# Rotary step of an interleaved diffusion trunk, split in two halves with its partner product behind the next chunk's projection

## The chip, the cores and the metric

The kernel runs on one core of one Trainium2 chip. The metric is the device time of one execution in microseconds (us). The kernel before has a median of 2652.2 us over 3 runs (2647.94 to 2653.35).

## What is computed

The reference is a trunk of four layers over 256 latent tokens and 256 context tokens of width 1024. Layers 0 and 3 mix tokens by differential attention, layer 1 by windowed grouped-query attention with sinks, layer 2 by a state-space scan; each mixer is followed by a gated feed-forward block. Only the rotary step of the attention layers is changed, and one multiplication in the differential softmax:

```
def apply_rope(t, cos, sin):
    t1, t2 = t[..., :half], t[..., half:]
    return jnp.concatenate([t1 * cs - t2 * sn, t2 * cs + t1 * sn], axis=-1)

q = apply_rope(qkv[..., :DA_WIDTH]..., cos, sin)      # latents only
k = apply_rope(qkv[..., DA_WIDTH:2 * DA_WIDTH]..., cos, sin)

p = jax.nn.softmax(s, axis=-1)
w = (p[:, :, 0] - lam * p[:, :, 1]).astype(v.dtype)
```

Context tokens get no rotation. In the last layer only latents are queried, but keys and values come from both streams.

## The kernel before

Activations lie feature-major: 8 chunks of 128 features by 512 tokens, the first 256 the context ("c"), the last 256 the latents ("l"). fp32 products are made of three matmuls on split operands: `uh`, `ul` are the rounded activation and its remainder, `wh`, `wl` the same of a weight. `load_w` fetches a 512 KB weight by DMA (SyncE's queue), rounds it on ScalarE (L261) and takes the remainder on GpSimd (L263).

An attention layer works in four groups of heads. A group has two key chunks and two query chunks (`qk_chunk`, a projection of 24 matmuls at L288 to L290 into a PSUM tile `mm` or `ar`), then the values (`v_tokens`, one token tile of 24 matmuls at L771 to L773 after the other), then the heads (`da_head`, `sw_head`). In layer 1 keys and values are made once, in group 0. In group 0 the two streams are projected apart (256 columns a matmul), later both at once (512 columns, except the queries of layer 3, which are latents only).

The latent half of a chunk is rotated by `rope`: ScalarE copies it to SBUF (`t`, L722), TensorE multiplies `t` by the matrix `rot` that swaps the partners (L724, into a PSUM tile `sm`), VectorE multiplies `t` by the cosine (L725) and the partner product by the sine (L726) and adds the two (L727, all in SBUF). `stack` then makes the operands of the score products: ScalarE writes the rounded halves (L701, L702), VectorE the remainder (L706 twice for keys, L712 for queries), and two DMAs move 64 partitions to the other half. The softmax of a head is L879 (maximum), L881 (exponential on ScalarE), L883, L884 (the second sum times minus lambda), L886, L887, and TensorE transposes the weights at L890. L471 to L475 are the normalisation of a head's output (`stat`), which ends in four transposes of `rs_y` at L475.

```
724         nc.tensor.matmul(rot[:, :HALF], self.cst["rot"], t, start=True, stop=True)
725         getattr(nc, self.ENG_ROPE).tensor_tensor(out=t, in0=t, in1=self.cst["cos"], op=AL.mult)
726         nc.vector.tensor_tensor(out=u, in0=rot[:, :HALF], in1=self.cst["sin"], op=AL.mult)
727         nc.vector.tensor_tensor(out=u, in0=u, in1=t, op=AL.add)
```

A scheduler orders each engine's instructions when the program is built. It mixes the next group's projections with the heads of the group at hand, so that a wait of one hides behind the other; once set, an engine's order is fixed. Tags of PSUM tiles have few buffers: `mm` 2 (and `ar` as a third in turn), `sm` 2 (in layer 3 `ad` as a third), `sc` 2. All 42 calls of `rope` (16 in layer 0, 10 in layer 1, 16 in layer 3) lie at 60 to 270, 760 to 900 and 2230 to 2380 us of the profiled execution.

Of the kernel before, what the change touches and what calls it, by code (L numbers as in the profile page):

```python
# [14 lines left out]
AL = mybir.AluOpType  # L15
AX = mybir.AxisListType

P = 128
D = 1024
KD = D // P  # L20
NT = 512
HALF = 256
# [12 lines left out]
def f32(ap):  # L35
    return ap.bitcast(F32)
# [139 lines left out]
class W:  # L176
    def __init__(self, h, l, kc, w):
        self.h, self.l, self.kc, self.w = h, l, kc, w


class Trunk:
# [28 lines left out]
    def __init__(self, ctx, tc, ins, outs, layers):  # L210
        self.tc, self.nc, self.ins, self.outs = tc, tc.nc, ins, outs
        self.layers = layers
        self.ctx = ctx
        pool = lambda n, **k: ctx.enter_context(tc.tile_pool(name=n, bufs=1, **k))
        self.main = pool("main")
        self.ps = pool("ps", space=bass.MemoryType.PSUM)
        self.dram = pool("dram", space=bass.MemoryType.DRAM)
        self.hs = None
        self.uid = 0
        self.poolw = set()  # L220
        self.wq, self.wloaded, self.wpos = [], {}, 0
        self.adaq = []
        self.adapend = []
        self.adaw = []
        self.extra, self.turn = None, {}
        self.arows = None

    def t(self, shape, tag, bufs=1, dt=F32, pool=None):
# [489 lines left out]
    def rope(self, src, scale):  # L718

        nc = self.nc  # L720
        t, u = next(self.vs), next(self.vs)
        nc.scalar.activation(t, src, AF.Copy, scale=scale)  # L722
        rot = self.psum("sm")
        nc.tensor.matmul(rot[:, :HALF], self.cst["rot"], t, start=True, stop=True)  # L724
        getattr(nc, self.ENG_ROPE).tensor_tensor(out=t, in0=t, in1=self.cst["cos"], op=AL.mult)  # L725
        nc.vector.tensor_tensor(out=u, in0=rot[:, :HALF], in1=self.cst["sin"], op=AL.mult)  # L726
        nc.vector.tensor_tensor(out=u, in0=u, in1=t, op=AL.add)  # L727
        return u

    def qk_chunk(self, wt, u, dst, kind, s):  # L730

        a, b = STREAMS[s]
        scale = 0.125 if kind == "q" else 1.0
        ps = self.psum("mm")
        self.lin(ps[:, : b - a], [(wt, range(KD))], 0, u[0], u[1], (a, b))
        if s != "l":
            self.stack(ps[:, :HALF], dst, kind, scale, slice(0, HALF))
        if s != "c":
            self.stack(self.rope(ps[:, b - a - HALF : b - a], scale), dst, kind, 1.0, slice(HALF, NT))

    def qk_tiles(self, tag, n, pool):

# [18 lines left out]
    def v_tokens(self, wv, u, dst, s):  # L761

        nc = self.nc
        a, b = STREAMS[s]
        mm = nc.tensor.matmul
        for tt in range(a // P, b // P):
            ps = self.psum("mm")
            tk = slice(tt * P, (tt + 1) * P)
            for k in range(KD):
                wt, kw = wv[k // 4], k % 4  # L770
                mm(ps[:, :HALF], u[0][k][:, tk], wt.h[:, kw, :], start=k == 0, stop=False)  # L771
                mm(ps[:, :HALF], u[1][k][:, tk], wt.h[:, kw, :], start=False, stop=False)  # L772
                mm(ps[:, :HALF], u[0][k][:, tk], wt.l[:, kw, :], start=False, stop=k == KD - 1)  # L773
            if dst[1] is None:
                nc.scalar.activation(dst[0][:, tt, :], ps[:, :HALF], AF.Copy)
            else:
                self.ctx_split(ps[:, :HALF], dst[0][:, tt, :], dst[1][:, tt, :])
# [83 lines left out]
    def da_head(self, hq, q, k, v, s, neg, pt4, pool):  # L861

        nc = self.nc
        a, b = STREAMS[s]
        nk = NT if s == "l" else HALF
        wth = self.t([P, 4, HALF], "wth", 1, F32R, pool=pool)
        wtl = self.t([P, 4, HALF], "wtl", 1, F32R, pool=pool)
        for qt in range(2):
            tk = slice(a + qt * P, a + (qt + 1) * P)
            mx = self.t([P, 2], "mx", 3)  # L870
            sm = self.t([P, 2], "sm", 3)
            pt = []
            pss = [self.psum("sc") for _ in range(2)]
            if self.PAIR:
                self.scores([ps[:, :nk] for ps in pss], q, k, range(2), tk, nk)
            for m, ps in enumerate(pss):
                if not self.PAIR:
                    self.scores([ps[:, :nk]], q, k, [m], tk, nk)
                nc.vector.tensor_reduce(out=mx[:, m : m + 1], in_=ps[:, :nk], axis=AX.X, op=AL.max, negate=True)  # L879
                p = next(pt4)  # L880
                nc.scalar.activation(p[:, :nk], ps[:, :nk], AF.Exp, bias=mx[:, m : m + 1], accum_out=sm[:, m : m + 1])  # L881
                pt.append(p)
            nc.vector.reciprocal(out=sm, in_=sm)  # L883
            nc.vector.tensor_tensor(out=sm[:, 1:2], in0=sm[:, 1:2], in1=neg, op=AL.mult)  # L884
            p0, p1 = pt[0][:, :nk], pt[1][:, :nk]
            nc.vector.tensor_scalar(out=p0, in0=p0, scalar1=sm[:, 0:1], scalar2=None, op0=AL.mult)  # L886
            nc.vector.scalar_tensor_tensor(out=p0, in0=p1, scalar=sm[:, 1:2], in1=p0, op0=AL.mult, op1=AL.add)  # L887
            tp = self.psum("sm")
            for kt in range(nk // P):
                nc.tensor.transpose(tp[:, kt * P : (kt + 1) * P], p0[:, kt * P : (kt + 1) * P], self.cst["ident"])  # L890
            src = tp[:, :nk].rearrange("p (k q) -> p k q", q=P)
            dh = wth[:, : nk // P, qt * P : (qt + 1) * P]
            dl = wtl[:, : nk // P, qt * P : (qt + 1) * P]
            nc.scalar.activation(dh, src, AF.Copy)
            nc.vector.tensor_tensor(out=dl, in0=src, in1=f32(dh), op=AL.subtract)
        ps = self.psum("sm")
        hc = slice(hq * P, (hq + 1) * P)
        n = nk // P
        for kt in range(n):
            self.mm3(  # L900
                ps[:, :HALF], v[0][:, kt, hc], v[1][:, kt, hc], wth[:, kt, :], wtl[:, kt, :],
                first=kt == 0, last=kt == n - 1,
            )
        return ps
# [104 lines left out]
    def sw_mixer(self, i, u, streams, pool, gate, after):  # L1009
        nc = self.nc  # L1010
# [10 lines left out]
        for g in range(4):  # L1021
            q = [self.qk_tiles("swq", self.SWQ, pool) for _ in range(2)]
            if g == 0:
                wk = [self.next_w(("swqk", i, c)) for c in range(2)]
                wq = [self.next_w(("swqk", i, 2 + c)) for c in range(2)]
                wv = [self.next_w(("swv", i, c)) for c in range(2)]
                for s in streams:
                    for c in range(2):
                        self.qk_chunk(wk[c], u, k[c], "k", s)
                    for c in range(2):  # L1030
                        self.qk_chunk(wq[c], u, q[c], "q", s)
                    self.v_tokens(wv, u, (v, None), s)
            else:
                for c in range(2):
                    self.qk_chunk(self.next_w(("swqk", i, 2 + 2 * g + c)), u, q[c], "q", "b")
            if g == 3:
                uo = self.u
                self.att_split(o, uo, range(6), streams)
            for s in streams:
                a, b = STREAMS[s]  # L1040
                n = 4 if s == "l" else 2
                for c in range(2):
                    wts = [
                        self.sw_head(4 * (2 * c + hr) + g, hr, q[c], k[c], s, sink, nsink, pt4, pool)
                        for hr in range(2)
                    ]
                    ps = self.psum("sm")

                    for kt in range(n):
                        for hr, wt in enumerate(wts):  # L1050
                            kv = 2 * c + hr
                            nc.tensor.matmul(
                                ps[64 * hr : 64 * hr + 64, :HALF], v[:, kt, 64 * kv : 64 * kv + 64], wt[:, kt, :],
                                start=kt == 0, stop=kt == n - 1, tile_position=(0, 64 * hr), skip_group_check=True,
                            )
                    nc.scalar.activation(o[2 * g + c][:, a:b], ps[:, :HALF], AF.Copy)
                if g == 3:
                    self.att_split(o, uo, (6, 7), s)
# [479 lines left out]
```

## Time and profile before

| what | value |
|---|---|
| median of 3 runs | 2652.2 us |
| profiled execution: its time, its span | 2648.17 us, 2646.2 us |
| TensorE matmul busy | 2495.8 us, 94% of the span |
| VectorE, ScalarE, GpSimd busy | 1538.5, 1212.5, 1113.6 us |
| mean granted TensorE clock | 0.983 |
| DMA | 353.29 MB, 134 GB/s on average |

TensorE is busy nearly throughout; the other engines have room on average. The span is the time from the first to the last instruction; some 2 us of the execution lie around it. A wait in the profile is idle time of an engine, put down to the instruction that ended it.

### The profile page before, as it was taken

What the parts mean: (1) busy time and instruction counts of PE and PEld (TensorE: products, weight loads), DVE (VectorE), ACT (ScalarE), POOL (GpSimd) and SP (SyncE); (2) the same over time, 40 slices, a digit from 0 to 9 for tenths busy, and PEclk for the clock granted to TensorE, in tenths of its full rate; (3) what the DMA queues carried; (4) which work ended last, traced back from release to release, by engine and by line L of the source; (5) the groups of instructions that cost most, each with busy time, mean ns of one, the idle gap of its engine ahead of it and who ended that gap; (6) DMA issues with size and microseconds to landing.
All of it is one profiled execution on the core that took longest, in us unless ns stands there. A gap on an engine that the chain in (4) does not pass through costs nothing. (4 is left out here: it accounts for less than half of the span.)

```text
span 2646.2 us, 37378 instructions
## 1 busy us (share of the span) xinstructions
PE 2495.8 (94%) x13570; PEld 2065.5 (78%) x13570; DVE 1538.5 (58%) x3797; ACT 1212.5 (46%) x2495; POOL 1113.6 (42%) x557
## 2 busy tenths in 40 slices
PE   7899999999989999999989899999999998997998
PEld 4777688888876688888877677678878887886997
DVE  3776658951467757961377777756673126766112
ACT  4555453222356753222356566645322225555443
POOL 3322035444241025444246556633544424433784
PEclk9999999999999999999999999999999998998999
DMA  8333427752141126752141121352684223333452
GB/s 319 126 102 129 144 90 250 259 179 96 64 150 45 53 72 235 254 172 96 52 139 57 64 76 56 101 179 77 201 310 159 97 76 128 97 93 121 162 186 76
DMA packets 108040, 353.29 MB, mean 134 GB/s; under 512 B 14032, under 2 KB 24656, under 8 KB 105808
## 3 DMA queue, kind: packets, MB, share of 16 engines
q1 hardware_dynamic: 107280, 349.57, 39.2%
q8 instruction: 107, 1.75, 0.3%
q10 hardware_dynamic: 576, 1.34, 0.1%
q14 instruction: 77, 0.63, 0.1%
HBM read 329.36 MB, written 11.53 MB: 129 GB/s over the span
## 5 line engine op out<-in xcount | busy, mean ns | idle before, releaser
L263 POOL TENSOR_TENSOR wl<-wr,wh 128x1024 fp32r<-128x1024 f32 x356 | 852.5, 2401 | 1339.2 <-ACT wh L261 1224.8
L261 ACT ACTIVATE wh<-wr 128x1024 fp32r<-128x1024 f32 x356 | 377.1, 1061 | 776.4 <-issue 278.6
L288 PE MATMUL mm<-uh,wh 128*128 128x512 f32 (+1 forms) x1184 | 423.7, 358 | 11.7 <-ACT uh L557 6.9
L289 PE MATMUL mm<-ul,wh 128*128 128x512 f32 (+1 forms) x1184 | 423.0, 357 | 0.6 <-DVE sublng L858 0.6
L290 PE MATMUL mm<-uh,wl 128*128 128x512 f32 (+1 forms) x1184 | 421.7, 356 | 0.0
L641 DVE TENSOR_TENSOR sc<-sc,sg 128x512 f32<-128x512 f32 (+1 forms) x100 | 57.6, 576 | 427.2 <-PE sc L290 420.3
L288 PE MATMUL sc<-uh,wh 128*128 128x512 f32 (+1 forms) x800 | 272.8, 341 | 0.7 <-DVE hid L644 0.7
L290 PE MATMUL sc<-uh,wl 128*128 128x512 f32 (+1 forms) x800 | 272.4, 341 | 0.0
L289 PE MATMUL sc<-ul,wh 128*128 128x512 f32 (+1 forms) x800 | 272.3, 340 | 0.0
L288 PEld LDWEIGHTS mm<-uh,wh 128*128 128x128 f32 x1184 | 228.2, 193 | 45.0 <-ACT uh L557 7.1
L289 PEld LDWEIGHTS mm<-ul,wh 128*128 128x128 f32 x1184 | 227.6, 192 | 30.4 <-issue 1.8
L290 PEld LDWEIGHTS mm<-uh,wl 128*128 128x128 f32 x1184 | 227.7, 192 | 29.9 <-issue 2.3
L298 PE MATMUL mm<-wh,hid 128*128 128x512 f32 x454 | 180.1, 397 | 0.9 <-DVE o L675 0.9
L300 PE MATMUL mm<-wl,hid 128*128 128x512 f32 x454 | 180.0, 397 | 0.0
L299 PE MATMUL mm<-wh,hid 128*128 128x512 f32 x454 | 179.7, 396 | 0.0
L288 PEld LDWEIGHTS sc<-uh,wh 128*128 128x128 f32 x800 | 152.1, 190 | 17.7 <-DVE hid L644 0.9
L290 PEld LDWEIGHTS sc<-uh,wl 128*128 128x128 f32 x800 | 151.9, 190 | 16.9
L289 PEld LDWEIGHTS sc<-ul,wh 128*128 128x128 f32 x800 | 151.8, 190 | 16.8
L387 DVE SCALAR_TENSOR_TENSOR sq<-wa,sm 128x512 f32<-128x512 f32 x224 | 145.4, 679 | 0.0
L263 POOL TENSOR_TENSOR wl<-wa,wh 128x1024 fp32r<-128x1024 f32 x49 | 117.7, 2403 | 59.7 <-ACT wh L261 57.0
L288 PE MATMUL ar<-uh,wh 128*128 128x256 f32 (+1 forms) x400 | 134.8, 337 | 1.9 <-ACT uh L557 1.9
L289 PE MATMUL ar<-ul,wh 128*128 128x256 f32 (+1 forms) x400 | 135.6, 339 | 0.0
(426 smaller groups left out, 5423.6 us busy)
## 6 DMA issues: line engine op xcount, KB each, us to landing
wr<-in_fin SPq DMA_DIRECT2D x154, 512.0 KB, 3.5
wa<-in_adat SPq DMA_DIRECT2D x144, 512.0 KB, 5.0
wr<-in_fout SPq DMA_DIRECT2D x77, 512.0 KB, 3.5
wr<-in_ssi SPq DMA_DIRECT2D x40, 512.0 KB, 3.5
wa<-in_adaw SPq DMA_DIRECT2D x36, 512.0 KB, 5.8
wr<-in_daqk SPq DMA_DIRECT2D x24, 512.0 KB, 3.9
wa<-in_fin SPq DMA_DIRECT2D x22, 512.0 KB, 3.5
wr<-in_sso SPq DMA_DIRECT2D x16, 512.0 KB, 3.5
```

The source lines that it names most:

```text
L261: nc.scalar.activation(h, raw, AF.Copy)
L263: eng.tensor_tensor(out=l, in0=raw, in1=f32(h), op=AL.subtract)
L288: mm(out, wh, ah[ka][:, a:b], start=j == 0, stop=False)
L289: mm(out, wh, al[ka][:, a:b], start=False, stop=False)
L290: mm(out, wl, ah[ka][:, a:b], start=False, stop=j == len(todo) - 1)
L298: mm(out, ah[ka][:, tk], wt.h[:, kw, :], start=j == 0, stop=False)
L299: mm(out, al[ka][:, tk], wt.h[:, kw, :], start=False, stop=False)
L300: mm(out, ah[ka][:, tk], wt.l[:, kw, :], start=False, stop=j == len(todo) - 1)
L387: nc.vector.scalar_tensor_tensor(out=self.t([P, D], "sq", 2)[:, :512], in0=w[:, x, :], scalar=1.0, in1=self.arows[r, x], op0=AL.mult, op1= ...
L641: nc.vector.tensor_tensor(out=pu[:, :w], in0=pu[:, :w], in1=sg[:, :w], op=AL.mult)
```

## The change

`rope` no longer returns a finished tile. It copies the latent half to SBUF as before, multiplies it by the cosine straight from the projection's PSUM tile (`w`, one instruction with the scale in it), and returns a function `rest`. That function holds the partner product, the product with the sine and the sum, both written in place to the PSUM tile; `stack` then reads the rotated chunk from PSUM. `qk_chunk` calls the previous chunk's `rest` and `stack` only after its own projection; the last query chunk's comes after the first token tile of the values, and in layer 1's later groups right behind the last query chunk. In the differential softmax the multiplication by minus lambda becomes a `tensor_scalar` with the factor as its scalar operand.

```diff
     def rope(self, src, scale):
 
         nc = self.nc
-        t, u = next(self.vs), next(self.vs)
+        t, w = next(self.vs), next(self.vs)
         nc.scalar.activation(t, src, AF.Copy, scale=scale)
-        rot = self.psum("sm")
-        nc.tensor.matmul(rot[:, :HALF], self.cst["rot"], t, start=True, stop=True)
-        getattr(nc, self.ENG_ROPE).tensor_tensor(out=t, in0=t, in1=self.cst["cos"], op=AL.mult)
-        nc.vector.tensor_tensor(out=u, in0=rot[:, :HALF], in1=self.cst["sin"], op=AL.mult)
-        nc.vector.tensor_tensor(out=u, in0=u, in1=t, op=AL.add)
-        return u
+        nc.vector.scalar_tensor_tensor(out=w, in0=src, scalar=scale, in1=self.cst["cos"], op0=AL.mult, op1=AL.mult)
+
+        def rest():
+            rot = self.psum("sm")[:, :HALF]
+            nc.tensor.matmul(rot, self.cst["rot"], t, start=True, stop=True)
+            nc.vector.tensor_tensor(out=rot, in0=rot, in1=self.cst["sin"], op=AL.mult)
+            nc.vector.tensor_tensor(out=rot, in0=rot, in1=w, op=AL.add)
+            return rot
+
+        return rest
...
-        if s != "c":
-            self.stack(self.rope(ps[:, b - a - HALF : b - a], scale), dst, kind, 1.0, slice(HALF, NT))
+        rest = self.rope(ps[:, b - a - HALF : b - a], scale) if s != "c" else None
+        self.turn_late()
+        if rest:
+            self.late = lambda: self.stack(rest(), dst, kind, 1.0, slice(HALF, NT))
+
+    def turn_late(self):
+        late, self.late = self.late, None
+        if late:
+            late()
...
             tk = slice(tt * P, (tt + 1) * P)
+            if tt == a // P + 1:
+                self.turn_late()
...
-            nc.vector.tensor_tensor(out=sm[:, 1:2], in0=sm[:, 1:2], in1=neg, op=AL.mult)
+            nc.vector.tensor_scalar(out=sm[:, 1:2], in0=sm[:, 1:2], scalar1=neg, scalar2=None, op0=AL.mult)
...
                     self.qk_chunk(self.next_w(("swqk", i, 2 + 2 * g + c)), u, q[c], "q", "b")
+                self.turn_late()
```

The built programs have as many instructions as before on SyncE, GpSimd, ScalarE, VectorE and TensorE, and differ in order only in and next to the three attention layers.

TensorE, layer 0, group 0, latents: the second query chunk is being projected into `mm`, and the partner product (L724, into `sm`) belongs to the first query chunk. Before:

```order
L290 MATMUL mm_144_730<-uh_13_84,wl_66_269 128x256
L288 MATMUL mm_144_730<-uh_13_84,wh_65_268 128x256
L289 MATMUL mm_144_730<-ul_14_85,wh_65_268 128x256
L724 MATMUL sm_143_720<-h_100_386,cst_att_93_370 128x256
L290 MATMUL mm_144_730<-uh_13_84,wl_66_269 128x256
L288 MATMUL mm_144_730<-uh_13_84,wh_65_268 128x256
```

In the change (the line numbers of the projection are one higher, the values' 15):

```order
L289 MATMUL mm_143_721<-uh_13_84,wh_65_268 128x256
L290 MATMUL mm_143_721<-ul_14_85,wh_65_268 128x256
L291 MATMUL mm_143_721<-uh_13_84,wl_66_269 128x256
L728 MATMUL sm_144_748<-h_100_386,cst_att_93_370 128x256
L786 MATMUL ar_145_757<-wh_68_274,uh_13_84 128x256
L787 MATMUL ar_145_757<-wh_68_274,ul_14_85 128x256
```

The partner product stood inside the next chunk's 24 projection matmuls, 11 behind their beginning; now it stands behind the last of them, in front of the first value tile.

VectorE, the same stretch, first and second key chunk. `h` is the SBUF scratch that `t`, `u` and `w` are cut from. Before:

```order
L726 TENSOR_TENSOR h_386<-sm_646,cst_att_370 128x256
L727 TENSOR_TENSOR h_386<-h_386 128x256
L706 TENSOR_TENSOR dk_389<-h_386,dk_387 64x256
L706 TENSOR_TENSOR dk_390<-h_386,dk_388 64x256
L725 TENSOR_TENSOR h_386<-h_386,cst_att_370 128x256
L726 TENSOR_TENSOR h_386<-sm_683,cst_att_370 128x256
L727 TENSOR_TENSOR h_386<-h_386 128x256
```

In the change:

```order
L724 SCALAR_TENSOR_TENSOR h_386<-ar_647,cst_att_370 128x256
L729 TENSOR_TENSOR sm_674<-sm_674,cst_att_370 128x256
L730 TENSOR_TENSOR sm_674<-sm_674,h_386 128x256
L707 TENSOR_TENSOR dk_389<-sm_674,dk_387 64x256
L707 TENSOR_TENSOR dk_390<-sm_674,dk_388 64x256
L1029 TENSOR_SCALAR nsink_6935<-sink_6934 128x16
L729 TENSOR_TENSOR sm_711<-sm_711,cst_att_370 128x256
L730 TENSOR_TENSOR sm_711<-sm_711,h_386 128x256
```

The cosine product of the second chunk (L724 of the change) has moved ahead of the first chunk's sine product; every instruction of the rotation now has one operand in PSUM.

ScalarE, the same stretch. Before:

```order
L722 ACTIVATE h_386<-mm_620 128x256
L261 ACTIVATE wh_1127<-wr_1126 128x1024
L701 ACTIVATE dk_387<-h_386 128x256
L702 ACTIVATE dk_388<-h_386 64x256
L722 ACTIVATE h_386<-ar_657 128x256
```

In the change:

```order
L723 ACTIVATE h_386<-mm_620 128x256
L262 ACTIVATE wh_1127<-wr_1126 128x1024
L723 ACTIVATE h_386<-ar_647 128x256
L262 ACTIVATE wh_1166<-wr_1165 128x1024
L702 ACTIVATE dk_387<-sm_674 128x256
L703 ACTIVATE dk_388<-sm_674 64x256
```

The second chunk's copy (L722, in the change L723) stood behind the first chunk's rounded halves; now it stands ahead of them.

## Rows read from the trace of the kernel before

**Rows 1.** The page's engines: busy us (share of the span) xinstructions.
```profile
PE 2495.8 (94%) x13570; PEld 2065.5 (78%) x13570; DVE 1538.5 (58%) x3797; ACT 1212.5 (46%) x2495; POOL 1113.6 (42%) x557
```
**Rows 2.** Layer 3's attention: length, busy us of PE, PEld, DVE, ACT, POOL, clock, DMA.
```profile
2220.00:2440.00 220.00, 186.75 (x1147) 161.81 (x1147) 146.42 (x319) 117.06 (x247) 83.35 (x44) 0.95 0.33 106
```
**Rows 3.** Waits of TensorE: line waited for, us in total, times, longest us.
```profile
PE sm L724 <- ACT h L722: 18.7, 15, 2.0
PE sm L475 <- DVE rs_y L442: 10.5, 7, 2.0
...
PE sm L890 <- DVE h L887: 5.8, 7, 1.4
...
PE ad L890 <- DVE h L887: 2.7, 1, 2.7
...
PE ad L724 <- ACT h L722: 2.0, 1, 2.0
```
**Rows 4.** Timeline, 73 to 79 us: start us, us, engine, line, out<-in [idle before <-releaser].
```profile
73.20 2.40 POOL L263 TENSOR_TENSOR wl<-wr,wh 128x1024 fp32r<-128x1024 f32 x1 [2.74 <-ACT wh L261]
...
73.62 2.26 DVE L727 TENSOR_TENSOR h<-h 128x256 f32<-128x256 f32 x1
...
75.92 0.42 ACT L701 ACTIVATE dk<-h 128x256 fp32r<-128x256 f32 x1 [2.79 <-DVE h L727]
...
77.76 0.37 ACT L722 ACTIVATE h<-mm 128x256 f32<-128x256 f32 x1
...
78.18 1.12 PE L724 MATMUL sm<-h,cst_att 128*128 128x256 f32 x2 [1.80 <-ACT h L722]
```
**Rows 5.** Instructions of L727, L726 and L712: duration ns min/median/max, first and last start, forms.
```profile
L727 DVE TENSOR_TENSOR h<-h x42: 417/425/2261, 68.6 to 2378.4; 128x256 f32<-128x256 f32 x42
...
L726 DVE TENSOR_TENSOR h<-sm,cst_att x38: 410/418/425, 68.1 to 2378.0; 128x256 f32<-128x256 f32 x38
...
L712 DVE TENSOR_TENSOR ql<-h,dq x16: 425/426/2414, 81.8 to 2379.3; 128x256 fp32r<-128x256 f32 x16
```
**Rows 6.** Busy time around three waits at L724 (columns as in rows 2; the clock fourth from the end).
```profile
74.00:78.30 4.30, 2.50 (x21) 2.29 (x21) 2.72 (x3) 2.16 (x4) 1.98 (x2) 1.00 0.65 215
78.40:81.70 3.30, 3.30 (x15) 3.12 (x15) 1.99 (x3) 0.31 (x1) 1.88 (x1) 0.50 0.36 82
...
774.70:778.00 3.30, 3.30 (x17) 3.24 (x16) 2.50 (x4) 1.10 (x3) 1.04 (x1) 0.50 0.37 105
...
2245.80:2249.10 3.30, 3.30 (x17) 3.30 (x17) 2.78 (x3) 0.66 (x2) 2.30 (x1) 0.50 0.11 29
```
**Rows 7.** Instructions of L884, L450 (a tensor_scalar of one column) and L1000, as rows 5.
```profile
L884 DVE TENSOR_TENSOR sm<-sm,neglam x48: 147/160/2218, 92.0 to 2407.9; 128x1 f32<-128x1 f32 x48
...
L450 DVE TENSOR_SCALAR rs_a<-rs_a x58: 204/214/217, 10.7 to 2639.5; 128x1 f32<-128x1 f32 x58
...
L1000 DVE TENSOR_SCALAR h<-h,sm x64: 342/476/2643, 790.9 to 918.0; 128x256 f32<-128x256 f32 x32, 128x512 f32<-128x512 f32 x32
```
**Rows 8.** Timeline of TensorE: two value matmuls of 256 columns, two projection matmuls of 512.
```profile
87.91 0.28 PE L772 MATMUL mm<-wh,ul 128*128 128x256 f32 x1
88.03 0.28 PE L773 MATMUL mm<-wl,uh 128*128 128x256 f32 x1
...
88.62 0.39 PE L288 MATMUL mm<-uh,wh 128*128 128x512 f32 x1
88.85 0.40 PE L289 MATMUL mm<-ul,wh 128*128 128x512 f32 x1
```
**Rows 9.** The stacked query's DMA (L715): time from issue to landing.
```profile
DMA to landing us min/median/max: 1.9/2.3/6.0
```
**Rows 10.** Timeline, layer 3: products of the second key and second query chunk, TensorE's wait.
```profile
2285.43 0.70 PE L724 MATMUL sm<-h,cst_att 128*128 128x256 f32 x2 [1.68 <-ACT h L722]
...
2289.05 0.70 PE L724 MATMUL sm<-h,cst_att 128*128 128x256 f32 x2 [0.35 <-ACT h L722]
```
**Rows 11.** What L724's engine waited for, us and times: L947 frees an `sm` tile.
```profile
  ACT o L947: 0.6, 3
```

More of the change, by code (lines that the diff above doesn't have):

```diff
@@ L225, in __init__ @@
         self.extra, self.turn = None, {}
+        self.late = None
         self.arows = None
```

## The prediction

> **What bounds the kernel now.** I read the engines' shares first: TensorE is busy for 94% of the span, VectorE for 58% [rows 1], so time is won where TensorE waits, and work taken off another engine counts only where TensorE waits for it. The stretches come next: in the attention of layer 3 TensorE is busy for 186.75 of 220 us [rows 2]; here, not in the feed-forward blocks, there is something to win. The list of waits says by what: TensorE waits at the rotary partner product L724 for ScalarE's copy L722, 15 times for 18.7 us and once for 2.0 us; these 20.7 us are the largest item that the change touches. Next to them stand the normalisation's transposes L475 (10.5 us) and the softmax's L890 (5.8 and 2.7 us) [rows 3].
>
> The timeline shows how such a wait comes about [rows 4]. GpSimd's weight remainder L263 starts at 73.20 and takes 2.40 us. VectorE's sum L727, with both inputs in SBUF, starts inside it at 73.62 and takes 2.26 us. ScalarE's L701 of the same chunk waits for that sum 2.79 us; behind it in ScalarE's order stands the next chunk's copy L722, which ends at 78.13, and TensorE, which came to L724 long before, has waited 1.80 us. The durations confirm the cause: L727 and L712, both with two SBUF inputs, have medians of 425 and 426 ns and maxima of 2261 and 2414, about the length of an L263; L726, with one input in PSUM, never exceeds 425 ns in 38 executions [rows 5]. So there are two faults here: VectorE is held up by GpSimd, and the product stands too early on TensorE for any delay to be absorbed.
>
> A longer wait also costs clock. After the 1.80 us wait the granted clock is 0.50 (1.2 of 2.4 GHz) from 78.4 to 81.7, where it was 1.00 before; the same level follows the two waits of 2.0 us, at 774.7 and 2245.8 [rows 6]. No other of these waits is followed so.
>
> **The change part by part.**
>
> *The product behind the next projection.* TensorE now meets it 24 matmuls later than the chunk's own end. A matmul starts 0.12 us after the last at 256 columns, 0.23 us at 512 [rows 8], so 2.9 or 5.5 us lie between; ScalarE's copy, 0.37 us long, has moved ahead of the previous chunk's L701 and no longer waits for the sum. The wait that needs most is the 2.0 us of rows 3, and before it the product already stood some matmuls into the next chunk. I take the whole 20.7 us as removed: **-20.7 us**. The bounds are 0 (all of it turns up elsewhere) and 20.7.
>
> *The clock.* Three stretches of 3.3 us at half clock did the work of 1.65 us each. Without a wait ahead of them I take them at full clock: 3 x 1.65 = **-5.0 us**; the bounds are 0 and 5.0, since the fall may come at another wait.
>
> *Sums and stacked parts from PSUM.* Each rotation keeps its count on VectorE: cosine, sine, sum, remainder. Now each has one PSUM input, like L726, so I expect 0.42 us each and no held-up ones. The profile has no sine product or sum written in place in PSUM; its price is bounded by L726's 410 and 425 ns [rows 5], and I take 418. What L727 and L712 lose to GpSimd goes from VectorE, but TensorE sees it only through the waits above: 0 beyond them.
>
> *Two readers on one bank.* The sine product, the sum, ScalarE's two halves and the remainder now follow each other on one `sm` tile: from the product to its release 0.7 + 0.42 + 0.42 + 0.4 + 0.4 + 0.42 (keys 0.84) = 2.8 to 3.2 us, where it was 0.7 + 0.42 + 0.42 = 1.5. With two buffers the second product after it wants the tile, two chunks later: 5.8 us of 256-column matmuls in group 0, about 5 us in layer 0's later groups, where the change puts 3 and then 20 projection matmuls of 512 columns between the first three products. So this is covered, with 2 us to spare. What a failing cover costs is the rival on the other side.
>
> *The last query chunk.* Its product now stands behind the first value tile, and its stacked part still has to land before the latents' scores: about 3 us to the DMA and 2.3 us to land [rows 9], 5.3 us. Three value tiles follow in the later groups (8.6 us), one in group 0 (2.9 us), where in layer 0 the context's scores come first; in layer 3 the first head needs only the first query chunk, whose product has two tiles behind it (5.8 us). Nothing for nearly all, up to 1 us once: 0.
>
> *Layer 3's later groups.* There the second key's product stood 11 matmuls into the second query chunk and still waited 1.68 us [rows 10]; it now stands at that chunk's beginning, 11 x 0.12 = 1.3 us earlier. It gains from projections that the new order starts earlier (seven of 512 columns, 1.6 us, before the first key's product instead of after it), so about 0.3 us may be left in each of three groups, here or at L475 behind it; the bounds are 0 and 1.7. **+1.0 us**.
>
> *Cover moved out of the heads.* In two of layer 0's groups six projections fewer stand before the last L475, 1.4 us each by 0.23 us a start. If TensorE waits there they are missed, if not they cost nothing: 0 to 2.8, and I take **+1.4 us**.
>
> *The multiplication by minus lambda.* L884 has a median of 160 ns and a maximum of 2218. A `tensor_scalar` on one column took 204 to 217 ns in 58 executions of L450, never held up. So it is 48 x 0.054 = 2.6 us more for VectorE, and the hold-ups go from this line. They do not go from the chain: directly behind stands L886, and L1000, the same operation on the same shapes, has been held up to 2643 ns [rows 7], so L886 inherits the wait. By L884's row alone the gain would reach the 2.7 us of TensorE's one long wait at L890 [rows 3]; by L1000's it is nothing. I take L1000's, and 0.05 us on each of 8 waits at L890: **+0.4 us**. The Trainium skill (SBUF — State Buffer, "Who interferes with whom") states that a VectorE instruction with two SBUF inputs contends with a GpSimd instruction that reads SBUF, and so does a `tensor_scalar` in its two-port mode: by it this edit moves the wait rather than ends it, the edits that read PSUM end it, and a sum from L884's row alone would be about 2.7 us lower. By that rule, the trace agrees: L727 at 2261 ns, L1000 at 2643, L726 at 425.
>
> The sum: -20.7 - 5.0 + 1.0 + 1.4 + 0.4 = -22.9 us. Against the profiled execution's 2648.2 us that is 2625.3. The median of the runs lies 4.0 us above this execution, which would give 2629.3; I forecast the middle, **2627 us**.
>
> **The rivals.**
>
> *Half comes back.* TensorE arrives earlier at the heads, but their softmax and normalisation chains on VectorE and ScalarE set the pace, and the time turns up at L475 and L890. For it: these lines already hold TensorE for 10.5 and 8.5 us [rows 3]. Against it: their inputs also come earlier, and VectorE is held up less. If 12 of the 25.7 us return, the gain is 11 and the time 2637 to 2641 us.
>
> *More than forecast.* VectorE's freed time also shortens L475 and L890, say by half of their 19 us: 2616 to 2620 us.
>
> *The rotary tile stays too long (slower).* The `sm` tile is shared with transposes, value products and normalisation. VectorE and ScalarE work in order; if the chain on the tile is stretched from 3 us beyond the 5 us between a product and the second one after it, TensorE waits at L728 or at a transpose. At 1.5 us for each of the 30 rotations outside group 0 that is 45 us against 25.7 gained: 19 slower, 2667 to 2671 us. Against it: L724 waited for an `sm` tile that L947 frees only 0.6 us in 3 times [rows 11]. It decides from a wait of 0.9 us per rotation (25.7 / 30).
>
> *No effect.* The products wait as before one chunk later, because ScalarE's copy is late for another reason (its order also carries the rounding of weights): 2648 to 2652 us.
>
> **How the numbers follow.** About 0.2%, 5.3 us, is what a measurement of this kernel can tell from no change. Forecast 0.55, half back 0.22, more 0.07, slower 0.08, no effect 0.08. Faster by over 0.2% are the first three, 0.84; within 0.2% 0.08; slower 0.08. The range takes in the forecast with its bounds (cover and layer 3 at their worst add 1.4 and 4.1 us, clock not won 5.0), the half-back case and most of the larger gain: 2614 to 2644. Outside lie the slower case, most of no effect, and the low end.
>
> **What would show it.** Right: waits of TensorE at the partner product of 2 us or less in all; none of the new sums above 0.5 us; no clock of 0.50 around the three places of rows 6; L886 with maxima above 2 us. Wrong: TensorE's waits at L475 and L890 (of the old numbering) grown by 10 us or more together; waits at the partner product put down to VectorE or to the release of `sm`; a span above 2640 us.

## The result and the profile after

The changed kernel takes 2624.4 us (median of 4 runs, 2623.08 to 2627.41) against 2652.8 us of the kernel before, run beside it: ratio 0.9892, 95% interval 0.988 to 0.9903. The profiled execution took 2624.96 us, with a span of 2623.1. The forecast was 2627 us, its range 2614 to 2644. The number came out; of the reasons a good part did not, as the runs below show.

The page's engines after, as [rows 1]:

```profile
PE 2489.5 (95%) x13570; PEld 2064.2 (79%) x13570; DVE 1511.0 (58%) x3797; ACT 1209.9 (46%) x2495; POOL 1114.4 (42%) x557
```

VectorE loses 27.5 us of busy time. The waits of TensorE after, as [rows 3] (the partner product is now L728, the normalisation's transposes L476, the transposes of the softmax weights L905):

```profile
PE ad L476 <- DVE rs_y L443: 7.2, 3, 2.4
...
PE sm L476 <- DVE rs_y L443: 5.6, 4, 1.9
PE ad L905 <- DVE h L902: 5.1, 4, 1.9
...
PE sm L728 <- ACT h L723: 4.5, 4, 1.4
...
PE sm L905 <- DVE h L902: 3.6, 6, 1.2
```

The product's 20.7 us are down to 4.5, but three waits of 2.4 us at L476, on tiles `ad`, are new: for these transposes `ad` stands in for `sm` in layer 3 alone. The sum L730, the remainder L713, the multiplication by minus lambda L899 and the scaling behind it L901, as [rows 5, 7] (the `sm` of L899 and L901 is the SBUF tile of the softmax sums, which shares its name with the PSUM tiles):

```profile
L730 DVE TENSOR_TENSOR sm<-sm,h x38: 416/432/433, 71.2 to 2359.9; 128x256 f32<-128x256 f32 x38
...
L713 DVE TENSOR_TENSOR ql<-sm,dq x12: 424/425/425, 78.8 to 2361.2; 128x256 fp32r<-128x256 f32 x12
...
L899 DVE TENSOR_SCALAR sm<-sm,neglam x48: 195/214/217, 86.7 to 2388.0; 128x1 f32<-128x1 f32 x48
...
L901 DVE TENSOR_SCALAR h<-h,sm x48: 343/478/2105, 86.8 to 2388.1; 128x512 f32<-128x512 f32 x32, 128x256 f32<-128x256 f32 x16
```

In this trace no operation that reads an operand from PSUM is held up, and L901 (L886 before, at most 484 ns there) has inherited what L899 lost; both as predicted. The clock, in stretches as [rows 2, 6] (busy time of PE, PEld, DVE, ACT, POOL; the clock is fourth from the end):

```profile
78.00:82.00 4.00, 4.00 (x34) 3.94 (x34) 2.05 (x5) 1.54 (x5) 2.11 (x1) 1.00 0.51 155
...
771.50:775.00 3.50, 3.50 (x21) 2.46 (x20) 1.95 (x7) 3.50 (x11) 0.00 (x0) 1.00 0.00 0
...
2253.40:2260.20 6.80, 5.56 (x24) 5.38 (x25) 3.50 (x9) 1.71 (x3) 0.64 (x1) 0.50 0.32 96
2200.00:2414.00 214.00, 186.41 (x1131) 162.95 (x1132) 137.63 (x298) 106.91 (x229) 81.60 (x44) 0.94 0.32 100
```

In layers 0 and 1 the two stretches at 0.50 of [rows 6] are gone. In layer 3 there is a longer one, and its attention is no shorter than before. The length of each attention is measured here from a transpose in the normalisation ahead of it (L541; L540 before; the same token tile in every kernel) to the first transpose of the one behind it. For layer 3, after:

```profile
2196.47 0.90 PE L541 MATMUL sm<-cst_base,sq 128*128 128x128 f32 x3 [5.67 <-ACT sq L537]
2413.53 0.90 PE L541 MATMUL ad<-cst_base,sq 128*128 128x128 f32 x4 [3.88 <-ACT sq L537]
```

That is 217.1 us. The same for every kernel of this study, from its profiled execution (us; "rest" is the span without the three; the time is the median of the runs):

| kernel | time | layer 0 | layer 1 | layer 3 | rest |
|---|---|---|---|---|---|
| before | 2652.8 | 291.4 | 200.7 | 210.5 | 1943.6 |
| after | 2624.4 | 273.5 | 190.2 | 217.1 | 1942.4 |
| e1 delay alone | 2642.2 | 289.7 | 193.9 | 208.3 | 1946.0 |
| e2 PSUM alone | 2625.3 | 282.6 | 194.6 | 202.5 | 1944.6 |
| e11 half of PSUM | 2629.6 | 284.6 | 193.7 | 204.1 | 1944.2 |
| e3 minus lambda undone | 2616.1 | 278.7 | 190.6 | 199.3 | 1945.7 |
| e4 no delay in layer 3 | 2619.5 | 273.8 | 190.4 | 206.4 | 1946.5 |
| e8 same order, other operation | 2629.9 | 274.4 | 190.4 | 217.7 | 1946.2 |
| e9 minus lambda alone | 2662.3 | 287.6 | 202.2 | 225.8 | 1948.9 |
| e5 inverse root in PSUM | 2612.1 | 272.7 | 191.3 | 201.5 | 1945.8 |
| e7 minus lambda in layer 0 only | 2610.6 | 272.5 | 190.7 | 199.1 | 1945.4 |
| e10 e5 and e7 | 2604.4 | 272.3 | 190.0 | 197.4 | 1942.5 |

The change gains 17.9 us in layer 0 and 10.5 in layer 1 and gives 6.6 back in layer 3. The rest differs by up to 6.5 us between kernels that are alike there; differences of a few us in the total are not explained by the stages.

How layer 3 gives time back stands in the timeline after, group 1 between its first and second key (all engines; start us, us):

```profile
2246.43 0.16 DVE L472 TENSOR_SCALAR rs_m<-sm 128x4 f32<-128x4 f32 x1
...
2246.76 2.40 POOL L264 TENSOR_TENSOR wl<-wa,wh 128x1024 fp32r<-128x1024 f32 x1 [7.63 <-ACT wh L262]
2246.88 2.31 DVE L435 TENSOR_SCALAR rs_y<-rs_m 128x4 int32<-128x4 int32 x1
...
2249.82 0.43 DVE L707 TENSOR_TENSOR dk<-mm,dk 64x256 fp32r<-64x256 f32 x1
...
2250.28 0.38 ACT L723 ACTIVATE h<-mm 128x256 f32<-128x256 f32 x1 [2.11 <-DVE dk L707]
...
2250.72 0.70 PE L728 MATMUL sm<-h,cst_att 128*128 128x256 f32 x2 [1.35 <-ACT h L723]
...
2251.69 2.35 POOL L264 TENSOR_TENSOR wl<-wr,wh 128x1024 fp32r<-128x1024 f32 x1 [2.53 <-ACT wh L262]
2251.85 2.21 DVE L442 TENSOR_TENSOR rs_a<-rs_a,rs_h 128x4 f32<-128x4 f32 x1
...
2254.43 0.15 DVE L443 SCALAR_TENSOR_TENSOR rs_y<-rs_a,rs_y 128x4 f32<-128x4 f32 x1
...
2254.64 1.11 PE L476 MATMUL ad<-cst_base,rs_y 128*128 128x128 f32 x4 [2.40 <-DVE rs_y L443]
```

L435 to L443 are the inverse root of the head normalisation (`rsqrt`), nine small VectorE operations. GpSimd's remainder L264 starts just before the first of them, and L435 takes 2.31 us in place of 0.17. Behind it in VectorE's order stands the remainder L707, for which ScalarE's copy L723 waits, and for that the partner product: 1.35 us. The next L264 holds up L442 for 2.21 us, and the transposes L476 wait 2.40. The same pair of waits comes in all three later groups, 11.3 us together. The stretch at half clock begins at 2253.4, inside the second wait of group 1.

### The profile page after: what moved, and what is told of

It reads as the page before. It is cut to its first block, busy times and chain, and to the rows that moved or that the text cites. A ratio compares the mean times of both kernels' runs of the same rounds, so it can differ in the third digit from the quotient of the medians.

```text
span 2623.1 us, 37393 instructions
## 1 busy us (share of the span) xinstructions
PE 2489.5 (95%) x13570; PEld 2064.2 (79%) x13570; DVE 1511.0 (58%) x3797; ACT 1209.9 (46%) x2495; POOL 1114.4 (42%) x557
## 5 line engine op out<-in xcount | busy, mean ns | idle before, releaser
L264 POOL TENSOR_TENSOR wl<-wr,wh 128x1024 fp32r<-128x1024 f32 x356 | 853.4, 2404 | 1297.2 <-ACT wh L262 1155.2
L289 PE MATMUL mm<-uh,wh 128*128 128x512 f32 (+1 forms) x1184 | 422.9, 357 | 11.3 <-ACT uh L558 6.9
L289 PE MATMUL sc<-uh,wh 128*128 128x512 f32 (+1 forms) x800 | 272.5, 341 | 0.8 <-DVE hid L645 0.6
L291 PE MATMUL sc<-uh,wl 128*128 128x512 f32 (+1 forms) x800 | 272.3, 340 | 0.0
L264 POOL TENSOR_TENSOR wl<-wa,wh 128x1024 fp32r<-128x1024 f32 x49 | 118.3, 2414 | 62.2 <-ACT wh L262 61.8
```

The costliest lines, as they stand in the source:

```text
L264: eng.tensor_tensor(out=l, in0=raw, in1=f32(h), op=AL.subtract)
L289: mm(out, wh, ah[ka][:, a:b], start=j == 0, stop=False)
L291: mm(out, wl, ah[ka][:, a:b], start=False, stop=j == len(todo) - 1)
```

## The experiments

A hold-up here is a VectorE operation that starts inside a GpSimd remainder and takes far longer than its median. Theory: hold-ups of VectorE by GpSimd are what costs, and the delay only makes room for them. Rivals: the product's place alone counts; the loss in layer 3 is the delay's; it is that of the multiplication by minus lambda, through its duration or through the order that the scheduler makes of it.

**e1, the delay alone.** The edits of `qk_chunk` and `v_tokens` stay; `rope` and L899 work as before:

```diff
+        def rest():
+            rot = self.psum("sm")
+            nc.tensor.matmul(rot[:, :HALF], self.cst["rot"], t, start=True, stop=True)
+            getattr(nc, self.ENG_ROPE).tensor_tensor(out=t, in0=t, in1=self.cst["cos"], op=AL.mult)
+            nc.vector.tensor_tensor(out=u, in0=rot[:, :HALF], in1=self.cst["sin"], op=AL.mult)
+            nc.vector.tensor_tensor(out=u, in0=u, in1=t, op=AL.add)
+            return u
```

> The delay alone: product and stack behind the next projection, but cosine, sine, sum and remainder from SBUF as before, and the multiplication by minus lambda as before. Theory 'placement' (the product stood too early on TensorE, the hold-ups of VectorE need not go): nearly the whole gain, 2624 to 2630 us, waits of TensorE at the product under 5 us although the sum still shows maxima of about 2.3 us. Theory 'lock' (only the end of the hold-ups by GpSimd counts): 2645 to 2653 us. If both parts are needed: 2632 to 2642 us, with waits at the product or at the scores left in between.

Measured: 2642.2 us, ratio 0.9965 (0.9952 to 0.9979), just past the upper end of "both needed". The sum and what waited for it (instructions of its line):

```profile
L730 DVE TENSOR_TENSOR h<-h x42: 410/426/2581, 71.6 to 2376.4; 128x256 f32<-128x256 f32 x42
...
  ACT dk L702: 33.8, 14
```

Delayed, the sum meets GpSimd more often: 17 of 42 are held up by over 0.5 us, before 7. TensorE's waits at the product fall to 8.4 us, but those at the scores grow (layer 3: 4.0 to 6.9 us; the 2.9 more are one wait for the DMA of a stacked query). Place alone does not do it.

**e2, the PSUM arithmetic alone.** L899 as before, and no delay:

```diff
-        self.turn_late()
         if rest:
-            self.late = lambda: self.stack(rest(), dst, kind, 1.0, slice(HALF, NT))
+            self.stack(rest(), dst, kind, 1.0, slice(HALF, NT))
```

> The PSUM arithmetic alone: cosine product from the projection's tile, sine product, sum and stacked parts in PSUM, but the product called at once as before; minus lambda as before. Theory 'placement': 2645 to 2653 us, TensorE still waits some 15 us at the product, now for the copy alone. Theory 'lock': 2624 to 2632 us, waits at the product under 5 us without any delay. Both needed: 2632 to 2645 us.

Measured: 2625.3 us, ratio 0.9903 (0.989 to 0.9917): as fast as the whole change. The product, still at its old place, waits 4.7 us:

```profile
PE sm L728 <- ACT h L723: 4.7, 14, 0.6
```

So 16 of the 20.7 us go without any delay. This is the "lock" theory's result.

**e11, half of it.** e2 with the sum written to SBUF, so that rounded parts and remainders come from there:

```diff
-            nc.vector.tensor_tensor(out=rot, in0=rot, in1=w, op=AL.add)
-            return rot
+            nc.vector.tensor_tensor(out=w, in0=rot, in1=w, op=AL.add)
+            return w
```

> The PSUM arithmetic alone without its second half: cosine product, sine product and sum read PSUM, but the sum is written to SBUF, and the rounded parts and the remainders are made from there, as before (no delay, minus lambda as before). In the kernel before, the held-up cosine products, sums and remainders lie at about 6, 13 and 18 us over their medians. If a hold-up counts for TensorE wherever it falls in the chain: about half of the 27 us, 2636 to 2642 us. If only the sum's hold-up reaches the next product: 2625 to 2630 us. If the remainder takes over the sum's hold-up (it is the next operation with two SBUF inputs): 2642 to 2652 us, with remainders held up more often than before.

Measured: 2629.6 us, ratio 0.9918 (0.9905 to 0.9932). The remainders are held up more than before: 16 of the 60 that read the sum, by 21.7 us over their median, where it was 9 and 17.3 us. One row for it:

```profile
L713 DVE TENSOR_TENSOR ql<-h,dq x16: 417/513/2411, 77.7 to 2360.3; 128x256 fp32r<-128x256 f32 x16
```

The cosine product and the sum carry some 22 of the 27 us; of the remainders' 21.7 us about 4 reach the time (e11 against e2). The time is that of the expectation's second case, though the third case's sign, more remainders held up, is there too.

**e3, minus lambda as before** (all else as in the change):

```diff
-            nc.vector.tensor_scalar(out=sm[:, 1:2], in0=sm[:, 1:2], scalar1=neg, scalar2=None, op0=AL.mult)
+            nc.vector.tensor_tensor(out=sm[:, 1:2], in0=sm[:, 1:2], in1=neg, op=AL.mult)
```

> The changed kernel with the multiplication by minus lambda as a tensor_tensor again. Prediction's step (the scaling behind it inherits the hold-up, so the edit moves a wait and saves none): within 2 us of the changed kernel, 2622 to 2626 us, with maxima of about 2.2 us back at this line and fewer held-up scalings. Rival (the edit ended hold-ups that TensorE waited for): 2 to 4 us slower, 2626 to 2629 us, and the transposes of the weights wait more.

Measured: 2616.1 us, ratio 0.9866 (0.9852 to 0.9879). Neither expectation: undoing the edit gains 8.2 us. Its hold-ups do behave as predicted:

```profile
L899 DVE TENSOR_TENSOR sm<-sm,neglam x48: 141/158/2201, 87.1 to 2375.5; 128x1 f32<-128x1 f32 x48
...
L901 DVE TENSOR_SCALAR h<-h,sm x48: 339/476/879, 88.7 to 2377.7; 128x512 f32<-128x512 f32 x32, 128x256 f32<-128x256 f32 x16
```

By the table the edit gains 5.2 us in layer 0 and costs 17.8 in layer 3. The order shows why it can: by the traces, the exchanged operation set aside, another instruction stands in 266 places of VectorE's order, 868 of TensorE's, 110 of ScalarE's and 4 of GpSimd's. Why the scheduler chose so is not shown. The timeline of e3 at the same place, group 1 of layer 3:

```profile
2250.52 0.17 DVE L435 TENSOR_SCALAR rs_y<-rs_m 128x4 int32<-128x4 int32 x1
...
2251.71 0.16 DVE L442 TENSOR_TENSOR rs_a<-rs_a,rs_h 128x4 f32<-128x4 f32 x1
...
2252.21 0.62 PE L476 MATMUL ad<-cst_base,rs_y 128*128 128x128 f32 x4
2252.55 2.39 POOL L264 TENSOR_TENSOR wl<-wa,wh 128x1024 fp32r<-128x1024 f32 x1 [6.50 <-ACT wh L262]
```

The inverse root runs in one go and is done before the next L264 begins. Neither product nor transposes wait.

**e4, no delay in layer 3's groups 1 to 3** (minus lambda as in the change):

```diff
             self.late = lambda: self.stack(rest(), dst, kind, 1.0, slice(HALF, NT))
+        if self.now:
+            self.turn_late()
...
+            self.now = g > 0 and not want_ctx
```

> The changed kernel, but in layer 3's groups 1 to 3 the product comes at once again. Theory 'the delay hurts there' (the second key's product stands at the start of the second query chunk with no cover and the normalisation's transposes right behind it, 3 x 1.4 and 3 x 2.4 us of waits that the kernel before did not have in this size): these waits fall to about the 6 us of before, and the time to about 2619 us. Rival 'GpSimd falls on the normalisation chain' (its instructions L435 and L442 are held up 2.3 and 2.2 us whatever the product does): the waits stay or move to other lines, and the time is 2622 to 2628 us.

Measured: 2619.5 us, ratio 0.9876 (0.9862 to 0.9889), exactly what "the delay hurts there" expected; the waits at L476 on `ad` are gone, the product waits 6.3 us in all. Yet e3, with the delay, has a shorter layer 3 (199.3 against 206.4), and e2, without delay and without the lambda edit, lies between (202.5). So the delay by itself does not hurt there; e4 changed the order too, and came upon a better one, in which L435 is still held up for 2.30 us in each of the three groups but L442 no longer. Its number fits a theory that falls.

**e8, the order of the change with another operation.** Whether order or operation costs:

```diff
-            nc.vector.tensor_scalar(out=sm[:, 1:2], in0=sm[:, 1:2], scalar1=neg, scalar2=None, op0=AL.mult)
+            nc.vector.scalar_tensor_tensor(out=sm[:, 1:2], in0=sm[:, 1:2], scalar=neg, in1=self.cst['ones'][:, 0:1], op0=AL.mult, op1=AL.mult)
```

> The changed kernel with the multiplication by minus lambda as a scalar_tensor_tensor whose second tensor is a column of ones in SBUF: the order of every engine stays word for word that of the changed kernel but for this operation's name, while the operation has two SBUF inputs again. Theory 'order' (the edit costs because the scheduler puts the normalisation's chain where GpSimd's remainders hold it up): about 2624 us, with three waits of 2.4 us at the normalisation's transposes in layer 3. Theory 'instruction' (a tensor_scalar with a scalar operand is the slow thing, by its length or by whom it passes the hold-up to): about 2616 us, without these waits.

Measured: 2629.9 us, ratio 0.991 (0.9898 to 0.9923). In the traces no engine's order differs from the change's but for this operation. It has two SBUF inputs again and is held up itself, L901 takes 804 ns at most, and the three waits stay:

```profile
L899 DVE SCALAR_TENSOR_TENSOR sm<-sm,neglam,cst_base x48: 199/219/1957, 87.1 to 2393.4; 128x1 f32<-128x1 f32 x48
```

```profile
PE ad L476 <- DVE rs_y L443: 7.2, 3, 2.4
```

Layer 3 takes 217.7 us, as in the change: the order costs there, not the operation. (Its 5 us over the change lie for the most part in the "rest" and are not explained.)

**e9, minus lambda alone on the kernel before** (the change's edit of that line, nothing else).

> The kernel before with nothing but the multiplication by minus lambda as a tensor_scalar. If the edit has a price of its own wherever it stands: 2658 to 2662 us (8 us more, as in the changed kernel). If its price is that of one order of the changed kernel, which the rotary step's place made: 2648 to 2655 us, or either way by a few us, with another pattern of waits at the normalisation's transposes.

Measured: 2662.3 us, ratio 1.0032 (1.0019 to 1.0044). Again layer 0 gains (3.8 us) and layer 3 loses (15.3), by three waits, longer still:

```profile
PE ad L475 <- DVE rs_y L442: 13.3, 3, 4.4
```

In each of these groups the inverse root again runs into two remainders: L434, its first operation here, takes 2.35 us, and L440 2.29. So the bad order came with this edit in both kernels, with the rotary step's change and without it.

**e5, the inverse root from PSUM** (minus lambda and delay as in the change). Mean, half mean and products lie in free columns of the sums' tile, and the squares are taken in two steps, so that no operation reads two SBUF tiles:

```diff
+            tt(out=a, in0=m, in1=y, op=AL.mult)
+            tt(out=a, in0=a, in1=y, op=AL.mult)
+            stt(out=b, in0=a, scalar=-10.0 / 3, in1=y, op0=AL.add, op1=AL.mult)
+            tt(out=a, in0=a, in1=b, op=AL.mult)
+            stt(out=y, in0=y, scalar=5.0, in1=a, op0=AL.mult, op1=AL.add)
+            tt(out=a, in0=mh, in1=y, op=AL.mult)
+            tt(out=a, in0=a, in1=y, op=AL.mult)
+            stt(out=y, in0=a, scalar=1.5 * 0.375, in1=y, op0=AL.add, op1=AL.mult)
...
+        if div == 128:
+            m, *sp = (ps[:, 8 * x : 8 * x + 2 * n] for x in range(1, 4))
```

> The changed kernel (minus lambda as a tensor_scalar in both layers) with the head normalisation's inverse root rewritten so that none of its operations reads two SBUF tiles: its mean, half mean and products lie in free columns of the PSUM tile of the sums, one operation more. Theory 'GpSimd on the normalisation chain': no operation of the chain exceeds 0.3 us, the waits of layer 3's groups 1 to 3 at the second key's product (1.4 us) and at the transposes (2.4 us) are gone, and the time is 2606 to 2614 us. Rival 'place' (the second key's product and the transposes stand too early on TensorE whatever VectorE is held up by): waits of over 1 us stay at both lines and the time is 2619 to 2625 us.

Measured: 2612.1 us, ratio 0.9842 (0.9826 to 0.9857). Layer 3 takes 201.5 us, 15.6 less. The first operation, with its input in PSUM in the heads and in SBUF in layer 2's four:

```profile
L435 DVE TENSOR_SCALAR rs_y<-sm x12: 143/157/161, 101.6 to 2380.1; 128x4 int32<-128x4 int32 x12
L435 DVE TENSOR_SCALAR rs_y<-rs_m x4: 162/1256/2346, 1458.3 to 1717.6; 128x4 int32<-128x4 int32 x4
```

The chain still meets the remainders, as the timeline of layer 3's group 1 shows (L446 is its last operation, L490 the transposes):

```profile
2248.18 2.40 POOL L264 TENSOR_TENSOR wl<-wa,wh 128x1024 fp32r<-128x1024 f32 x1 [7.64 <-ACT wh L262]
...
2248.30 0.15 DVE L435 TENSOR_SCALAR rs_y<-sm 128x4 int32<-128x4 int32 x1
...
2252.86 0.15 DVE L446 SCALAR_TENSOR_TENSOR rs_y<-sm,rs_y 128x4 f32<-128x4 f32 x1
...
2253.16 0.62 PE L490 MATMUL ad<-cst_base,rs_y 128*128 128x128 f32 x4
```

L435 starts 0.12 us into L264, as in the change, and takes 0.15 us. In the three groups 21 of the chain's operations start inside a remainder, none takes over 171 ns, and no wait is left at the product or at L490. So it is not a luckier order that helps here. Both that and e7 (below) remove the loss in layer 3, one by taking the chain out of GpSimd's reach, the other by its place: the mechanism is shown from two sides.

**e7, minus lambda as a tensor_scalar in layer 0 only** (in layer 3 as before):

```diff
+            if self.ts_lam:
+                nc.vector.tensor_scalar(out=sm[:, 1:2], in0=sm[:, 1:2], scalar1=neg, scalar2=None, op0=AL.mult)
+            else:
+                nc.vector.tensor_tensor(out=sm[:, 1:2], in0=sm[:, 1:2], in1=neg, op=AL.mult)
```

> The changed kernel with the multiplication by minus lambda as a tensor_scalar in layer 0 and as a tensor_tensor in layer 3. By the stages of the runs so far the edit gains 5.2 us in layer 0 (273.5 us of attention against 278.7) and costs 17.7 in layer 3 (217.0 against 199.3). If the two are independent: 2616.1 - 5.2 = about 2611 us, which is faster than every kernel so far. If layer 0's difference is not the edit's, but chance of the order: about 2616 us.

Measured: 2610.6 us, ratio 0.9841 (0.9827 to 0.9854), as expected.

**e10, e7 with e5's inverse root.**

> The changed kernel with minus lambda as a tensor_scalar in layer 0 only and with the inverse root of the head normalisation reading PSUM. If the two win the same hold-ups (the three places of layer 3 that each of them freed): no faster than the better one alone, 2609 to 2612 us. If the rewritten root wins something of its own in layer 0 and at the last group: 2603 to 2607 us.

Measured: 2604.4 us, ratio 0.9828 (0.9814 to 0.9841), the fastest of all: 47 us under the kernel before, run beside it. In layer 0 the last wait at the normalisation's transposes (here L490; 1.9 us in e7) goes too; what is left lies in layer 2, whose root still reads SBUF:

```profile
PE sm L490 <- DVE rs_y L454: 3.6, 3, 1.6
```

Its stages are 0.2 to 1.7 us shorter than e7's, the rest 2.9, and the runs overlap (2604.16 to 2610.18 against 2609.86 to 2613.06), so how much over e7 is its own stays open.

## Why the prediction was right, and where it was not

For the balance, each attention's length is split into TensorE's gaps of over 0.06 us, the time lost at half clock (half of the time at 0.50 outside these gaps) and what remains; sums over layers 0, 1 and 3:

| kernel | length | gaps | lost clock | remainder |
|---|---|---|---|---|
| before | 702.6 | 61.3 | 16.3 | 625.0 |
| e2 | 679.7 | 42.1 | 11.7 | 625.9 |
| e3 | 668.6 | 37.5 | 10.9 | 620.2 |
| after | 680.8 | 45.5 | 16.7 | 618.6 |

- *The product behind the next projection, -20.7.* Right for the rotary step without the lambda edit: e3 waits 0.2 us there, once. But the cause was given mostly to the place; by e2 the PSUM arithmetic removes 16 us of it, and by e1 the delay alone 12. The change as a whole keeps 4.5 us, more than twice the 2 us set as a sign.
- *The clock, -5.0.* Right in e3 (10.9 against 16.3, 5.4 less), wrong in the change: 16.7, no less than before, since layer 3's new waits bring stretches of their own.
- *PSUM arithmetic, 0 beyond these waits.* The price of the operations was right (432 ns against 418). "0 beyond" was too small: of the 22.9 us that e2 gains in the three attentions, 16 are the product's waits, 4.6 the clock, and 3 lie in other gaps (the remainder takes back 0.9). Both parts of the rotary edit (e3) gain 34.0 us there where 25.7 were expected: 3.1 of the 8.3 more are other gaps, 4.8 are the remainder of the table, which is not explained.
- *Two readers on one bank, 0.* Right: no kernel's product waits more than 0.3 us for an `sm` tile to be released, and the rival built on it is out.
- *Layer 3's later groups, +1.0.* The place was right, the cause and size wrong. The product waits 1.4 us there, not 0.3, and the transposes 2.4 us, but with the same delay e3 has neither.
- *Cover moved out of the heads, +1.4.* Not seen: layer 0's waits at the last transposes fell from 6.9 us to 4.9 in e3 and 1.9 in the change.
- *Minus lambda, +0.4.* **This step failed**: the edit costs 8.2 us. That the hold-up passes to the next operation was right (L901 at 2105 ns). The Trainium skill (SBUF — State Buffer, "Who interferes with whom") states that a VectorE instruction with two SBUF inputs contends with a GpSimd instruction that reads SBUF; the traces agree, with e8's operation at 1957 ns and the change's L899 at 217. Two inputs are not the only case: L435 reads one SBUF tile and was held up for 2.31 us. But the step priced an operation in a fixed order. The scheduler moved some hundreds of others for it, and in layer 3 put the normalisation's inverse root across two of GpSimd's remainders.

So the forecast held by luck, by two errors of opposite sign: by the medians the rotary step gains 36.2 us (-23.3 expected), the lambda edit costs 8.2 (+0.4). The delay and PSUM parts are worth about 10 and 27 us alone (e1, e2) and 36 together, so they all but add up, and the delay has a share of its own that the theory at the head of the experiments denied it; the change shows 28 of the 36. None of the rivals held: waits at L476 and L905 grew by 2.5 us together, not by 10. Of the signs for being right, two held (no sum above 0.5 us, scalings above 2 us), the clock's held in two places of three, and the product's waits did not.

## What to carry to other kernels

Where a scheduler sets the order, price a small edit by the rows that it moves on every engine before pricing the operation itself, and look there for chains that now overlap another engine's long operations. A chain of small VectorE operations on the way to TensorE is as exposed to GpSimd as a wide one: give each a PSUM operand where a tile has columns free. Delaying the consumer is a second means, worth 10 us here with the hold-ups in place (e1) and 9 with those of the rotary step gone (e3 against e2). Test an edit's parts from more than one side, since one experiment can return the expected number through another change of order (e4).

## What the runs showed of the hardware

Small operations are held up as long as wide ones: four columns of int32 for 2.31 us in place of 0.17, one column with two SBUF inputs for 1957 ns at a median of 219; a `tensor_scalar` of one column never passed 217 ns in 48 executions. Written in place in PSUM, the sums cost 432 ns, 7 more than in SBUF without a hold-up. Where the sum stayed in SBUF, the delay made its hold-ups more frequent, 17 in place of 7, since at the later place it starts more often inside a remainder (19 of 42 sums, before 7); the kernel was 10 us faster all the same.
